# Low halves of weights and operand pairs made by an accumulating DMA in place of VectorE differences

## The chip, the cores and the metric

The kernel runs on one core of one Trainium2 chip. The metric is the time of one execution on the device in microseconds; the verdict compares medians of several runs. In the profile PE is TensorE (PEld its weight loads), DVE is VectorE, ACT is ScalarE, POOL is GpSimd, and SP is the engine whose queue issues most loads.

## The reference

A trunk of two layers over 512 tokens of 1024 channels in float32. Each layer has a mixing part (a combined projection, four branches, gates, an output projection, a residual add), and behind it a feed-forward part, in which the change lies:

```python
def _conv_ffn(h, w_up, conv_w, conv_b, w_down):
    u = _depthwise_conv(h @ w_up, conv_w, conv_b)      # width 3, along the tokens
    gate, up = jnp.split(u, 2, axis=-1)
    return (jax.nn.silu(gate) * up) @ w_down
...
x = x + _conv_ffn(_rmsnorm(x, g_ffn[l]), w_up[l], ffn_conv_w[l], ffn_conv_b[l], w_down[l])
```

`w_up` is 1024 x 5632 (22 blocks of 128 gate channels and 22 of up channels), `w_down` is 2816 x 1024.

## The kernel before

**Products in two halves.** TensorE works on the type fp32r, which keeps fewer bits than float32. Each operand x is therefore split: a high part hi = x rounded to fp32r, and a low part lo = x - hi. A product is three matmuls, hi*hi, hi*lo and lo*hi, summed in PSUM (`prod`, lines 291 to 296). ScalarE makes the high part by a copy, VectorE makes the low part by a subtraction.

**Weights.** `weights` (line 243) prepares the entries of `w_list` in their order, always two ahead of the one in use (`unit`, `LOOK = 2`). For a plain entry it loads 512 KB on SP's queue into `w_raw` (two buffers), makes `w_hi` on ScalarE (line 273) and `w_lo` on VectorE (line 275); `w_hi` and `w_lo` have three buffers each, so the tile of block k can be written when TensorE is done with block k-3. An entry is a pair (n, pieces); n is 1024 for plain blocks, 0 for entries of the down-projection, and 'seven' for the entries below, which `seven_unit` prepares (lines 1276 and 1277), where further operands are added to a raw tile in place by an accumulating DMA on GpSimd's queue (`grow`, line 1258).

**Up-projection.** `ffn` (line 1190) walks `UP_STEPS`. Blocks 2 to 15 are computed in pairs of blocks by a seven-product scheme (`seven`, line 1111); blocks 0, 1 and 16 to 21 are whole: `block` (line 312) makes 24 matmuls of 512 columns for the gate half (s = 0) and the same for the up half (s = 1). VectorE takes each result from its bank into `U` (line 1215); there are four banks named mm and four named aux. Then `conv_part` (line 1163) does the width-3 convolution: one ScalarE step (line 1171) and two VectorE steps (1172, 1173), for s = 0 a Silu on ScalarE (1177), for s = 1 the product with it (1185). The result for blocks 2j and 2j+1 lies side by side in one tile `f` with the tag `fp{j}`, 128 x 1024.

**Down-projection.** `down` (line 1369) also works by seven products, on pairs j = 0 to 10. Each needs operands made from f by `split_pair` (line 1329): four VectorE steps of 256 columns (sums and differences of the quarters of the two blocks), and splits into hi and lo of both blocks, of the sum tile `a` (512 columns) and of a quarter `b` (256 columns): ScalarE at line 1354, VectorE at line 1355. Pairs 0 to 5 are done early, still in the up-projection, behind blocks 15 to 20 (`EARLY`); pairs 6 to 10 at the start of the first steps of `down`. The low parts of pair j go into the buffer of the pair before, `fp{j-1}`; those of pair 0 into the tag `lo`.

**What sets the order.** Tile, the framework, fixes the order of instructions on each engine when the kernel is built, by priorities: work on weights comes with a high priority (`high_priority`), and engines run their list in that order and wait at semaphores. A buffer with a tag is written again only after its last reader is done.

Of the kernel before, what the change touches and what calls it, by code (L numbers as in the profile page):

```python
# [14 lines left out]
F32 = mybir.dt.float32  # L15
F32R = mybir.dt.float32r
I32 = mybir.dt.int32
AF = mybir.ActivationFunctionType
ALU = mybir.AluOpType
# [3 lines left out]
P = 128  # L23
L = 2
D = 1024
S = 512
KT = D // P
NB = S // P
DFF = 2816
# [31 lines left out]
              ('gb', 'A22'), ('ga', 'S2'), ('ga', 'S1'), ('gb', 'S2'), ('gb', 'S1'), ('ga', 'S4'), ('gb', 'S4')]  # L61
MIX = (0, 1, 4, 5, 2, 3, 6, 7)

EARLY = (15, 16, 17, 18, 19, 20)
EPS = 1e-6
BIG = 1e30
EB = 4
# [167 lines left out]
class Trunk:  # L235
# [7 lines left out]
    def weights(self, upto, ahead=3000, parts=1, queue=None):  # L243

        nc = self.nc
        while self.w_emitted < min(upto, len(self.w_list)):
            n, pieces = self.w_list[self.w_emitted]
            if n == 'seven':
                with self.tc.high_priority(offset=ahead):
                    self.w_ready.append(self.seven_unit(*pieces))  # L250
                self.w_emitted += 1
                continue
            with self.tc.high_priority(offset=ahead):

                self.w_fast = (self.w_fast + 1) % 4 if n == 0 else 0
                if n == 0 and self.w_fast in (3, 0):
                    raw = self.fp.tile([P, 1024], F32, name="w_raw", tag="w_more", bufs=2)
                else:
                    raw = self.wpool.tile([P, 1024], F32, name="w_raw", tag="w_raw", bufs=2)
                hi = self.wpool.tile([P, 1024], F32R, name="w_hi", tag="w_hi", bufs=3)  # L260
                lo = self.wpool.tile([P, 1024], F32R, name="w_lo", tag="w_lo", bufs=3)
                src = pieces()
                n = sum(p.shape[1] for p in src)
                if len(src) == 1:
                    cut = [slice(i * n // parts, (i + 1) * n // parts) for i in range(parts)]
                    src = [src[0][:, s] for s in cut]
                c = 0
                for p in src:
                    (queue or nc.sync).dma_start(raw[:, c:c + p.shape[1]], p)
                    c += p.shape[1]  # L270
                for i in range(parts):
                    s = slice(i * n // parts, (i + 1) * n // parts)
                    w = nc.scalar.activation(hi[:, s], raw[:, s], AF.Copy)  # L273
                    self.first_hi = self.first_hi or w
                    nc.vector.tensor_tensor(lo[:, s], raw[:, s], hi[:, s].bitcast(F32), ALU.subtract)  # L275
            self.w_ready.append((hi, lo))
            self.w_emitted += 1

# [884 lines left out]
    def conv_part(self, i, s):  # L1163

        nc = self.nc
        v = nc.vector
        c = i + s * NF
        u = self.U[s][:, i % 2]
        y = self.fp.tile([P, S], F32, name=f"cy{s}", tag=f"cy{s}", bufs=2)
        w = lambda t: self.par('ffn_conv_w', c * 3 + t)  # L1170
        nc.scalar.activation(y, u[:, 1:513], AF.Identity, scale=w(1), bias=self.par('ffn_conv_b', c))  # L1171
        v.scalar_tensor_tensor(y, u[:, 0:512], w(0), y, ALU.mult, ALU.add)
        v.scalar_tensor_tensor(y, u[:, 2:514], w(2), y, ALU.mult, ALU.add)

        if s == 0:
            si = self.fp.tile([P, S], F32, name="fth", tag="fth", bufs=2)
            nc.scalar.activation(si, y, AF.Silu)
            self.silus[i] = si
            return
        if self.last and i % 2 == 1 and i // 2 < KT:  # L1180
            self.turn_res(i // 2)
        if i % 2 == 0:
            self.fpair = self.fp.tile([P, 1024], F32, name="f", tag=f"fp{i // 2}", bufs=1)
        fl = self.fpair[:, i % 2 * S:(i % 2 + 1) * S]
        v.tensor_tensor(fl, y, self.silus.pop(i), ALU.mult)
        self.F.append(fl)
        if i in EARLY:
            self.split_pair(self.F, EARLY.index(i), self.got)

    def ffn(self, l, last):  # L1190
        nc = self.nc
        v = nc.vector
        self.U = []
        for i in range(2):
            u = self.conv_tile(f"U{i}")
            nc.gpsimd.memset(u[:, :, 0:1], 0.0)
            nc.gpsimd.memset(u[:, :, 513:514], 0.0)
            self.U.append(u)
        self.F, self.got, self.silus, self.sevens, self.last = [], {}, {}, {}, last
        held = {}  # L1200
        self.pace = 0.0
        for kind, a, b in UP_STEPS:
            if kind == 'seven':
                self.seven(a, b)
                continue
            if kind == 'free':
                ps = held.pop((a, b))
            else:
                ps = self.mm()
                self.block(ps)  # L1210
                self.tick()
            if kind == 'held':
                held[a, b] = ps
            else:
                v.tensor_tensor(self.U[b][:, a % 2, 1:513], ps, self.RB, ALU.mult)  # L1215
                self.conv_part(a, b)
        for g in self.slow:
            for _ in g:
                pass
        self.slow = []  # L1220
        return self.F
# [107 lines left out]
    def split_pair(self, F, j, got):  # L1329

        nc = self.nc
        v = nc.vector
        fi, fk = F[2 * j:2 * j + 2]

        def tile(t):
            if isinstance(t, tuple):
                t, n = t
                if n == 0:
                    pool = self.fp2 if t[:2] == "lt" else self.fp
                    self.halves[t] = pool.tile([P, 1024], F32R, name=f"p{t}", tag=t, bufs=1)  # L1340
                return self.halves[t][:, n * S:(n + 1) * S]
            pool = self.xpool if t[:2] in ("xh", "xl") else self.fp2 if t[:2] in ("fh", "t2", "t3") else self.fp
            return pool.tile([P, S], F32R, name=f"p{t}", tag=t, bufs=2 if t in ("lo", "xr", "xn", "cy0", "cy1") else 1)

        tags = self.pair_tags(j)
        ih, kh, il, kl, ah, al = (tile(t) for t in tags[:6])
        if j % 2 == 0:
            got['b'] = [tile(t) for t in tags[6:]]
        lo, hi = slice(0, 256), slice(256, 512)
        bh, bl = (t[:, (lo, hi)[j % 2]] for t in got['b'])  # L1350
        a = self.fp.tile([P, S], F32, name="sum", tag="xr" if j < len(EARLY) else "fth", bufs=2)

        def split(h, l, x):
            nc.scalar.activation(h, x, AF.Copy)
            v.tensor_tensor(l, x, h.bitcast(F32), ALU.subtract)

        v.tensor_tensor(a[:, lo], fi[:, hi], fk[:, hi], ALU.subtract)
        v.tensor_tensor(fi[:, hi], fi[:, lo], fi[:, hi], ALU.subtract)
        v.tensor_tensor(a[:, hi], a[:, lo], fi[:, lo], ALU.subtract)
        split(ih, il, fi)  # L1360
        split(ah, al, a)
        split(kh, kl, fk)
        v.tensor_tensor(fk[:, lo], fk[:, lo], a[:, hi], ALU.add)
        split(bh, bl, fk[:, lo])
        cut = lambda h, l, c: [(h[:, c + b * P:c + (b + 1) * P], l[:, c + b * P:c + (b + 1) * P]) for b in range(2)]
        got[j] = {'a11': cut(ih, il, 0), 's1': cut(ih, il, 256), 'a12': cut(kh, kl, 0), 's4': cut(kh, kl, 256),
                  's3': cut(ah, al, 0), 's2': cut(ah, al, 256), 'a22': cut(bh, bl, 0)}

    def down(self, F, last):
# [9 lines left out]

        got, todo = self.got, list(range(len(EARLY), NP2))  # L1380
        A, B = ([self.mm() for _ in range(2)] for _ in range(2))
# [94 lines left out]
    def run(self):  # L1476
        nc, tc = self.nc, self.tc
        with ExitStack() as st:
            pool = lambda name, **k: st.enter_context(tc.tile_pool(name=name, bufs=1, **k))
# [9 lines left out]
            for l in range(L):  # L1489
                off, quads, quarters, ups, mixing = 0, [], {}, {}, []  # L1490
                for kind, a, n in UNITS:
                    src = self.W[l, off:off + n * P].rearrange("(p c) -> p c", p=P)
# [16 lines left out]
                for kind, a, b in UP_STEPS:  # L1509
                    if kind == 'seven':  # L1510
                        self.w_list.append((kind, (l, a, b)))
                    elif kind != 'free':
                        self.w_list.append((1024, lambda src=ups[b * DFF + a * P]: [src]))
                self.quarters.append(quarters)
                self.quads.append(quads)
                self.sums.append([])
# [12 lines left out]
            with tc.tile_pool(name="first", bufs=1, reuse_waits="tile") as first:  # L1529
# [11 lines left out]
                for d in range(KT):  # L1541
                    if d == 0:
                        xn = x0[:, KT:]
                        for s in (slice(0, KT + 256), slice(KT + 256, KT + S)):
                            nc.sync.dma_start(x0[:, s], self.X0[:, s])
                    else:
                        xn = first.tile([P, S], F32, name="xn", tag="xn", bufs=7)
# [163 lines left out]
```

## Time and profile before

| | |
|---|---|
| median of 3 runs | 1548.46 us (1544.78 to 1549.47) |
| the profiled execution | 1549.1 us, span of its instructions 1547.3 us |
| granted TensorE clock | 1.000 |
| GpSimd issues of line 1258 | 72 (54 into chain, 18 into w_raw) |
| loads of 512 KB into w_raw on SP's queue | 187 of W, median 4.4 us to landing |
| HBM read / written | 258.20 MB / 58.72 MB |

Busy time is the time in which an engine has an instruction under way, so stages with different limits are averaged in the page's first line; the windows by stage tell them apart. A busy TensorE may still be held up between two matmuls by less than the view shows, as the ends of matmuls are modelled. The time to landing runs from the start of the issuing instruction to the transfer's last semaphore event.

### The profile page before, as it was taken

The page shows a single profiled execution, that of the slowest core. Times are in us where ns is not written, and L with a number is a line of the kernel's source. Part 1 is how long each engine was busy: PE and PEld are TensorE (multiplying, and loading weights), DVE is VectorE, ACT ScalarE, POOL GpSimd, SP SyncE. Part 2 cuts the span into 40 slices and gives each one's busy share as a digit, 9 for nine tenths or more (in the row PEclk, how much of TensorE's full clock was granted, in tenths as well). Part 3 has the DMA queues.
Part 4 walks back from the last instruction along what each step waited for, and adds up shares of the span by engine and source line. Part 5 has one row for each costly group of instructions (what it writes and reads, how often), then busy time and mean ns, then how long its engine had stood idle before and what let it go on. Part 6 is the DMA issues. An engine that isn't in the chain of part 4 may idle for free.

```text
span 1547.3 us, 23306 instructions
## 1 busy us (share of the span) xinstructions
PE 1530.9 (99%) x8446; PEld 1325.7 (86%) x8446; DVE 1308.3 (85%) x2220; ACT 953.0 (62%) x1600; POOL 185.9 (12%) x280
## 2 busy tenths in 40 slices
PE   9999999999999999999999999999999999999998
PEld 8888888889889998878888888888898899998787
DVE  6689988797879989996576899887988789999974
ACT  6677777356655666564548687673566565665643
POOL 0123002220001110000002130023200011100000
PEclk9999999999999999999999999999999999999999
DMA  7789586756558886366558796866665699863664
GB/s 233 235 224 200 164 177 157 177 153 152 177 142 179 190 169 159 95 209 198 180 184 254 206 197 175 170 160 182 147 152 177 171 216 213 173 164 95 188 223 157
DMA packets 116739, 277.57 MB, mean 179 GB/s; under 512 B 27280, under 2 KB 29200, under 8 KB 116624
## 3 DMA queue, kind: packets, MB, share of 16 engines
q1 hardware_dynamic: 86800, 186.93, 37.7%
q0 software_dynamic: 29536, 88.62, 31.1%
q8 instruction: 67, 1.10, 0.3%
q10 hardware_dynamic: 288, 0.52, 0.1%
q14 instruction: 48, 0.39, 0.1%
HBM read 258.20 MB, written 58.72 MB: 205 GB/s over the span
## 4 chain that ended last, share of the span: by engine, by line
PE 69%; DVE 16%; DMA 6%; ACT 5%; issue 4%; SPq 0%; POOL 0%; ACTq 0%; DVEq 0%; POOLq 0%
PE mm L294 11%; PE mm L295 11%; PE mm L296 11%; PE aux L1128 5%; DVE w_lo L1277 4%; DMA chain<-W 4%; PE aux L948 3%; PE aux L1378 3%; PE aux L1377 3%; PE aux L1376 3%; DVE w_lo L275 2%; PE mm L1376 2%; PE mm L1378 2%; PE mm L1377 2%; DMA w_raw<-W 2%
## 5 line engine op out<-in xcount | busy, mean ns | idle before, releaser
L273 ACT ACTIVATE w_hi<-w_raw 128x1024 fp32r<-128x1024 f32 (+1 forms) x233 | 241.9, 1041 | 198.1 <-PE aux L1378 51.0
L275 DVE TENSOR_TENSOR w_lo<-w_raw,w_hi 128x1024 fp32r<-128x1024 f32 (+1 forms) x233 | 280.5, 1206 | 72.5 <-ACT w_hi L273 71.3
L294 PE MATMUL mm<-xh,w_hi 128*128 128x512 f32 x704 | 275.6, 391 | 0.0
L295 PE MATMUL mm<-xl,w_hi 128*128 128x512 f32 x704 | 274.6, 390 | 0.0
L296 PE MATMUL mm<-xh,w_lo 128*128 128x512 f32 x704 | 274.5, 390 | 0.0
L1128 PE MATMUL aux<-form,w_hi 128*128 128x256 f32 x896 | 160.8, 280 | 0.7 <-ACT sv L1140 0.7
L296 PEld LDWEIGHTS mm<-xh,w_lo 128*128 128x128 f32 x704 | 132.2, 188 | 28.3
L294 PEld LDWEIGHTS mm<-xh,w_hi 128*128 128x128 f32 x704 | 132.2, 188 | 26.3
L295 PEld LDWEIGHTS mm<-xl,w_hi 128*128 128x128 f32 x704 | 132.3, 188 | 25.9
L1128 PEld LDWEIGHTS aux<-form,w_hi 128*128 128x128 f32 x896 | 137.5, 188 | 1.7 <-ACT sv L1140 1.1
L1128 PE MATMUL aux<-form,w_lo 128*128 128x256 f32 x448 | 125.9, 281 | 0.0
L1277 DVE TENSOR_TENSOR w_lo<-chain,w_hi 128x1024 fp32r<-128x1024 f32 x72 | 87.9, 1220 | 32.2 <-ACT w_hi L1276 28.6
L1276 ACT ACTIVATE w_hi<-chain 128x1024 fp32r<-128x1024 f32 x72 | 76.0, 1056 | 61.4 <-DMA chain<-W 27.8
L469 DVE SCALAR_TENSOR_TENSOR cv<-cv,prm 128x512 f32<-128x512 f32 x120 | 94.7, 789 | 0.7
L1171 ACT ACTIVATE cy<-U,prm 128x512 f32<-128x512 f32 x88 | 67.9, 808 | 40.6 <-DVE U L1215 30.3
L1258 POOL DMA_DIRECT2D chain<-W x54 | 47.3, 876 | 328.9 <-DVE w_lo L1277 296.8
L1128 PEld LDWEIGHTS aux<-form,w_lo 128*128 128x128 f32 x448 | 84.1, 188 | 0.4 <-DVE w_lo L1277 0.4
L1276 ACT ACTIVATE w_hi<-w_raw 128x1024 fp32r<-128x1024 f32 x54 | 56.7, 1054 | 43.8 <-PE aux L1128 18.2
L532 PE MATMUL mm<-w_hi,xh 128*128 128x512 f32 x192 | 76.4, 398 | 0.3 <-DVE V L660 0.3
L533 PE MATMUL mm<-w_lo,xh 128*128 128x512 f32 x192 | 74.9, 390 | 0.0
L534 PE MATMUL mm<-w_hi,xl 128*128 128x512 f32 x192 | 74.9, 391 | 0.0
L1277 DVE TENSOR_TENSOR w_lo<-w_raw,w_hi 128x1024 fp32r<-128x1024 f32 x54 | 65.8, 1219 | 6.0 <-ACT w_hi L1276 4.6
(372 smaller groups left out, 3900.2 us busy)
## 6 DMA issues: line engine op xcount, KB each, us to landing
w_raw<-W SPq DMA_DIRECT2D x187, 512.0 KB, 4.4
chain<-W POOLq DMA_DIRECT2D x54, 512.0 KB, 5.7
sums<-W POOLq DMA_DIRECT2D x24, 1024.0 KB, 12.0
w_raw<-W SPq DMA_DIRECT2D x66, 256.0 KB, 3.8
w_raw<-sums SPq DMA_DIRECT2D x44, 256.0 KB, 3.8
w_raw<-sums SPq DMA_DIRECT2D x22, 512.0 KB, 4.3
sums<-W POOLq DMA_DIRECT2D x12, 768.0 KB, 10.3
chain<-W SPq DMA_DIRECT2D x18, 512.0 KB, 5.0
```

Source lines behind the costliest of these rows:

```text
L273: w = nc.scalar.activation(hi[:, s], raw[:, s], AF.Copy)
L275: nc.vector.tensor_tensor(lo[:, s], raw[:, s], hi[:, s].bitcast(F32), ALU.subtract)
L294: mm(ps, lhsT=wh, rhs=xh, start=start, stop=False)
L295: mm(ps, lhsT=wh, rhs=xl, start=False, stop=False)
L296: self.last_mm = mm(ps, lhsT=wl, rhs=xh, start=False, stop=stop)
L469: self.after_mm(v.scalar_tensor_tensor(acc, u[:, t:t + S], w(t), acc, ALU.mult, ALU.add))
L1128: self.last_mm = nc.tensor.matmul(o, lhsT=w[:, s], rhs=x, start=start and not (e or j or i), stop=j == 3 and i == 2, skip_group_check=True)
L1276: nc.scalar.activation(hi, raw, AF.Copy)
L1277: nc.vector.tensor_tensor(lo, raw, hi.bitcast(F32), ALU.subtract)
L1376: mm(ps, lhsT=x[0], rhs=w[0][:, cols], start=start, stop=False, skip_group_check=again)
L1377: mm(ps, lhsT=x[0], rhs=w[1][:, cols], start=False, stop=False, skip_group_check=again)
L1378: self.last_mm = mm(ps, lhsT=x[1], rhs=w[0][:, cols], start=False, stop=stop, skip_group_check=again)
```

## The change

Two groups of low parts are no longer VectorE differences. ScalarE writes minus the high part into the low tile, and an accumulating DMA on GpSimd's queue adds the original values to it, from HBM for weights and from the tile f in SBUF for pairs: lo = -hi + x.

The weights are those of the whole blocks 18 to 21, both halves, in each layer: their entry carries n = 2 in place of 1024, and `weights` reads it as a flag.

The pairs are the six early ones. `early_pair` replaces `split_pair` for them: one high part of 128 x 1024 in place of two of 128 x 512, one negation, one DMA. The quarter b is written to a further tile of the tag `xr` and no longer into f, which the DMA reads. `EARLY` now names the block and the half behind which a pair is made: pair 1 moves from behind block 16 to behind the first half of block 17.

```diff
-EARLY = (15, 16, 17, 18, 19, 20)
+EARLY = ((15, 1), (17, 0), (17, 1), (18, 1), (19, 1), (20, 1))
...
-                src = pieces()
+                src, summed = pieces(), n == 2
...
                     w = nc.scalar.activation(hi[:, s], raw[:, s], AF.Copy)
                     self.first_hi = self.first_hi or w
-                    nc.vector.tensor_tensor(lo[:, s], raw[:, s], hi[:, s].bitcast(F32), ALU.subtract)
+                    if summed:
+                        nc.scalar.activation(lo[:, s], hi[:, s].bitcast(F32), AF.Copy, scale=-1.0)
+                        nc.gpsimd.dma_start(lo[:, s], src[i], accum_op=ALU.add)
+                    else:
+                        nc.vector.tensor_tensor(lo[:, s], raw[:, s], hi[:, s].bitcast(F32), ALU.subtract)
...
             self.silus[i] = si
+            if (i, 0) in EARLY:
+                self.early_pair(EARLY.index((i, 0)))
...
-        if i in EARLY:
-            self.split_pair(self.F, EARLY.index(i), self.got)
+        if (i, 1) in EARLY:
+            self.early_pair(EARLY.index((i, 1)))
+
+    def early_pair(self, j):
+
+        nc = self.nc
+        v = nc.vector
+        f = self.fpairs[j]
+        tags = self.pair_tags(j)
+        hi = self.fp2.tile([P, 1024], F32R, name="pfh", tag=f"fh{j}", bufs=1)
+        low = self.fp.tile([P, 1024], F32R, name="plo", tag=f"fp{j - 1}" if j else "lo", bufs=1)
+        ah, al = (self.pair_tile(t) for t in tags[4:6])
+        if j % 2 == 0:
+            self.got['b'] = [self.pair_tile(t) for t in tags[6:]]
+        bh, bl = (t[:, j % 2 * 256:j % 2 * 256 + 256] for t in self.got['b'])
+        a = self.fp.tile([P, S], F32, name="sum", tag="xr", bufs=2)
+        q = lambda n: f[:, n * 256:(n + 1) * 256]
+        v.tensor_tensor(a[:, :256], q(1), q(3), ALU.subtract)
+        v.tensor_tensor(q(1), q(0), q(1), ALU.subtract)
+        nc.scalar.activation(hi, f, AF.Copy)
+        nc.scalar.activation(low, hi.bitcast(F32), AF.Copy, scale=-1.0)
+        nc.gpsimd.dma_start(low, f, accum_op=ALU.add)
+        v.tensor_tensor(a[:, 256:], a[:, :256], q(0), ALU.subtract)
+        b = self.fp.tile([P, S], F32, name="sum", tag="xr", bufs=2)[:, :256]
+        v.tensor_tensor(b, q(2), a[:, 256:], ALU.add)
+        nc.scalar.activation(ah, a, AF.Copy)
+        v.tensor_tensor(al, a, ah.bitcast(F32), ALU.subtract)
+        nc.scalar.activation(bh, b, AF.Copy)
+        v.tensor_tensor(bl, b, bh.bitcast(F32), ALU.subtract)
...
-                        self.w_list.append((1024, lambda src=ups[b * DFF + a * P]: [src]))
+                        self.w_list.append((2 if a >= 18 else 1024, lambda src=ups[b * DFF + a * P]: [src]))
```

`pair_tile` is the function `tile` that stood inside `split_pair`, moved out so that both can use it; `split_pair` still serves pairs 6 to 10. `fpairs` is a list of the tiles f. `pair_tags`, which names the buffers, is unchanged.

More of the change, by code (lines that the diff above doesn't have):

```diff
@@ L1183, in conv_part @@
             self.fpair = self.fp.tile([P, 1024], F32, name="f", tag=f"fp{i // 2}", bufs=1)
+            self.fpairs.append(self.fpair)
         fl = self.fpair[:, i % 2 * S:(i % 2 + 1) * S]
@@ L1186, in conv_part @@
         self.F.append(fl)
-        if i in EARLY:
-            self.split_pair(self.F, EARLY.index(i), self.got)
+        if (i, 1) in EARLY:
[25 more added lines that the diff above has]
+        v.tensor_tensor(bl, b, bh.bitcast(F32), ALU.subtract)
+        cut = lambda h, l, c: [(h[:, c + b * P:c + (b + 1) * P], l[:, c + b * P:c + (b + 1) * P]) for b in range(2)]
+        self.got[j] = {'a11': cut(hi, low, 0), 's1': cut(hi, low, 256), 'a12': cut(hi, low, 512),
+                       's4': cut(hi, low, 768), 's3': cut(ah, al, 0), 's2': cut(ah, al, 256), 'a22': cut(bh, bl, 0)}
@@ new lines, in pair_tile @@
+    def pair_tile(self, t):
+        if isinstance(t, tuple):
+            t, n = t
+            if n == 0:
+                pool = self.fp2 if t[:2] == "lt" else self.fp
+                self.halves[t] = pool.tile([P, 1024], F32R, name=f"p{t}", tag=t, bufs=1)
+            return self.halves[t][:, n * S:(n + 1) * S]
+        pool = self.xpool if t[:2] in ("xh", "xl") else self.fp2 if t[:2] in ("t2", "t3") else self.fp
+        return pool.tile([P, S], F32R, name=f"p{t}", tag=t, bufs=2 if t in ("xr", "xn", "cy0", "cy1") else 1)
@@ L1199, in ffn @@
         self.F, self.got, self.silus, self.sevens, self.last = [], {}, {}, {}, last
+        self.fpairs = []
         held = {}
@@ L1333, in split_pair @@
         fi, fk = F[2 * j:2 * j + 2]
[L1335 to L1343, printed above, removed]
+        tile = self.pair_tile
         tags = self.pair_tags(j)
```

## The prediction

> **What bounds the kernel now.** I read the page's busy line first, then busy time by stage, then the end of the up-projection instruction by instruction.
>
> ```profile
> span 1547.3 us, 23306 instructions
> PE 1530.9 (99%) x8446; PEld 1325.7 (86%) x8446; DVE 1308.3 (85%) x2220; ACT 953.0 (62%) x1600; POOL 185.9 (12%) x280
> q0 software_dynamic: 29536, 88.62, 31.1%
> ```
>
> TensorE is busy for all but 1547.3 - 1530.9 = 16.4 us, so nothing that relieves another engine can return more than that, and only where the wait ends there. The stages that the edit touches are the end of the up-projection (606 to 664 us in layer 0, 1374 to 1437 in layer 1) and the down-projection behind each. The next rows give, after each window, its length, the busy time of PE, PEld, DVE, ACT and POOL, the granted clock, the share of the 16 DMA engines, and GB/s.
>
> ```profile
> 450.00:600.00 150.00, 148.96 (x1187) 145.58 (x1186) 133.31 (x171) 92.83 (x116) 23.61 (x27) 1.00 0.81 178
> 606.00:664.00 58.00, 58.00 (x269) 48.51 (x268) 57.94 (x94) 34.62 (x51) 0.00 (x0) 1.00 0.34 101
> 612.00:658.00 46.00, 46.00 (x205) 38.10 (x204) 45.96 (x76) 23.26 (x35) 0.00 (x0) 1.00 0.34 102
> 664.00:724.00 60.00, 59.19 (x258) 48.11 (x257) 51.90 (x91) 34.74 (x46) 0.00 (x0) 1.00 0.68 222
> 1374.00:1437.00 63.00, 63.00 (x291) 52.62 (x290) 62.94 (x102) 39.65 (x59) 0.00 (x0) 1.00 0.35 109
> 1437.00:1497.00 60.00, 59.74 (x260) 48.48 (x259) 50.06 (x75) 33.92 (x44) 0.00 (x0) 1.00 0.68 212
> ```
>
> VectorE is full there (57.94 of 58, 62.94 of 63), but TensorE never waits: 58.00 of 58, 63.00 of 63. VectorE keeps up exactly. The list of TensorE's waits shows where its backlog surfaces, and what else TensorE waits for on VectorE:
>
> ```profile
> PE aux L948 <- DVE w_lo L1277: 3.1, 4, 0.8
> ...
> PE aux L1128 <- DVE w_lo L1277: 1.3, 3, 0.6
> ...
> PE mm L1376 <- DVE U L1215: 1.1, 2, 0.8
> ```
>
> The third row is the one: at the start of each down-projection a product needs a bank that VectorE empties late, two waits, 1.1 us in all. The other two lie in stages that the edit leaves alone.
>
> **VectorE, what goes.** The groups of 606 to 664 us, one row for each kind of work:
>
> ```profile
> L275 DVE TENSOR_TENSOR w_lo<-w_raw,w_hi 128x1024 fp32r<-128x1024 f32 x11 | 13.4, 1218 | 0.0
> L1355 DVE TENSOR_TENSOR pfp<-f,pfh 128x512 fp32r<-128x512 f32 x9 | 6.0, 683 | 0.0
> L273 ACT ACTIVATE w_hi<-w_raw 128x1024 fp32r<-128x1024 f32 x11 | 11.5, 1047 | 1.3 <-PE mm L295 1.3
> L1354 ACT ACTIVATE pfh<-f 128x512 fp32r<-128x512 f32 x7 | 4.3, 627 | 5.5 <-DVE f L1358 5.5
> ```
>
> Eight blocks (18 to 21, both halves) a layer lose 1.218 us each: 9.7. Six pairs lose two differences of 0.683 each: 8.2. The other VectorE steps of a pair keep their count and size. So 17.9 us a layer leave an engine that has none to spare, and the backlog at the down-projection goes: I credit both of its waits, -1.1 us. Next behind it is the product's own rate; nothing more comes back here, because TensorE waits for nothing else.
>
> **ScalarE, what is added.** Eight negations of 1.047 us (8.4), and for each pair two instructions of 1.047 in place of two of 0.627 (6 x 0.84 = 5.0): 13.4 us, so 48.0 of 58. It fits; 13.4 us of ScalarE's idle time there was waiting for VectorE, by the same list:
>
> ```profile
> L1171 ACT ACTIVATE cy<-U,prm 128x512 f32<-128x512 f32 x14 | 10.9, 810 | 13.4 <-DVE U L1215 12.8 <-DVE U L1153 0.7
> ```
>
> **GpSimd's queue and the latency of a weight.** GpSimd is idle in the stage (0.00) and gets 14 issues a layer. The nearest rows are the growing operand sums of line 1258, also accumulating DMAs of 512 KB into SBUF:
>
> ```profile
> L1258 POOL DMA_DIRECT2D chain<-W x54: 863/872/909, 328.8 to 1361.4; - x54
> ...
> DMA to landing us min/median/max: 5.1/5.7/9.8
> ```
>
> 14 x 0.872 = 12.2 us of issuing, hidden. The landing isn't free: the low part now comes 1.047 + 5.7 us after the high part, where it was 1.218. Low-part tiles rotate over three buffers, so block k's is free when block k-3 is done, and its first use is the third product of block k:
>
> ```profile
> 615.28 1.06 ACT L273 ACTIVATE w_hi<-w_raw 128x1024 fp32r<-128x1024 f32 x1 [1.31 <-PE mm L295]
> 626.59 0.39 PE L296 MATMUL mm<-xh,w_lo 128*128 128x512 f32 x1
> 632.96 1.05 ACT L273 ACTIVATE w_hi<-w_raw 128x1024 fp32r<-128x1024 f32 x1
> 642.91 0.39 PE L296 MATMUL mm<-xh,w_lo 128*128 128x512 f32 x1
> ```
>
> First pair of rows: 615.28 + 1.06 + 1.05 + 5.7 = 623.1, needed at 626.59, 3.5 us to spare. Second, where ScalarE comes late: 640.8 against 642.91, 2.1 to spare. So a median landing hides; the longest seen (9.8) would stop TensorE by 0.6 to 2.0 us. I use 2.8 us as the mean slack.
>
> The Trainium skill would put this landing lower: "DMA: Bandwidth & Descriptors", section "Anatomy of one DMA — SWDGE (gpsimd) path", fits 2.0 us plus bytes / 436 GB/s, 3.2 us for 512 KB. By that the slack is 5.3 us and the sum is -1.1 us. The 5.1 to 9.8 us above speak against it for accumulating transfers.
>
> **The DMA engines.** This decides the sign. A window with one accumulate and nothing else large, one with a plain load of the same 512 KB, and a crowded one:
>
> ```profile
> 330.40:334.20 3.80, 3.80 (x19) 3.18 (x19) 3.23 (x5) 3.00 (x4) 0.00 (x0) 1.00 0.88 141
> 618.50:621.70 3.20, 3.20 (x16) 2.65 (x15) 3.20 (x6) 2.17 (x3) 0.00 (x0) 1.00 0.56 164
> 1251.00:1260.00 9.00, 9.00 (x78) 9.00 (x78) 8.53 (x12) 6.61 (x10) 2.62 (x3) 1.00 1.04 214
> ```
>
> The accumulate holds all 16 engines for 0.88 x 3.80 = 3.34 us, a plain load for 0.56 x 3.20 = 1.79. Three values for an accumulate: 3.34 alone; 2.85 from the software queue's line (88.62 MB in 31.1% of 1547.3 us is 184 GB/s, but plain copies are among them); and from 450 to 600 us, where 27 of them share the engines with loads: 178 GB/s x 150 us = 26.7 MB, less 14.2 MB of accumulates leaves 12.5 MB of loads, at 164/0.56 = 293 GB/s 42.8 us; (0.81 x 150 - 42.8) / 27 = 2.91 us. I take 2.91, since that stage is the most alike. A pair's accumulate reads SBUF where these read HBM; no row shows one. Bounds: 1.79, the plain load, and 3.34.
>
> The accumulates that the products wait for, or that lie ahead of those in the queue, are the eight weights and the pairs between the first and the last (four of six; the first can go before, the sixth is wanted in the down-projection). They fall into 612 to 658 us: 12 x 2.91 = 34.9 us, and 0.34 x 46 = 15.6 us are there already: 50.5 us of work in 46. Short by 4.5, of which 2.8 is slack: 1.7 us of stall a layer, 3.4 in both. With 2.85: 49.8, 1.0 a layer. With 3.34: 55.7, 6.9 a layer. With pairs at 1.79: 8 x 2.91 + 4 x 1.79 + 15.6 = 46.0, none. The crowded window, at a share of 1.04, kept PE at 9.00 of 9, so a short overload is carried.
>
> Of waits that the edit adds: a pair's negation writes the buffer of the pair before, so it waits until that pair's DMA has landed, and ScalarE's next high part is queued behind it. Blocks are (642.91 - 626.59) / 3 = 5.44 us apart, negation and landing take 1.05 + 5.7 = 6.7, and only pairs 1 and 2 are one block apart: 1.3 us, inside the 2.1, nothing. GpSimd's queue has nothing else that waits. In the down-projection the share is 0.68, with room for the last pair. Pair 1 moves from block 16 to the first half of block 17, one product later, and its first use is two weight tiles into the down-projection: nothing. On SP's queue the next raw load can start earlier, since ScalarE's high part is now the raw tile's last reader: nothing, loads land before they are wanted (ScalarE waits for PE in the row at 615.28, not for a load).
>
> **Sum.** -1.1 + 3.4 = +2.3 us: 1549.1 for the profiled execution (span 1547.3 and 1.8 around it) becomes 1551.4; the median of the runs shown, 1548.46, is 0.6 lower, so 1550.8. A measurement here tells about 0.3% from no change, 4.6 us: my forecast is "within", at +0.15%.
>
> **Rivals**, each from the median 1548.46.
> Slower, the DMA engines fill. Same place, 612 to 658 us and its twin in layer 1, with 3.34 us for each accumulate: 2 x 6.9 - 1.1 = +12.7 us, 1561.2. It leaves the 0.3% when an accumulate costs more than (46 + 2.8 + 2.85 - 15.6) / 12 = 3.0 us, close to my 2.91. For it: 3.34 was measured alone, and pairs queue ahead of weights in one queue. Against: 2.91 was measured in company, and 1.04 did no harm. The Trainium skill's rule behind it, "DMA: Bandwidth & Descriptors", section "Issuing engines are not separate DMA queues", is that all issuers' transfers run interleaved on the same 16 engines; the crowded window's share agrees. Chance 0.34.
>
> Slower, ScalarE blocked. With a landing of 9.8 us between pairs 1 and 2 it stands 1.05 + 9.8 - 5.44 = 5.4 us, 3.3 over the slack, a layer: +6.6 - 1.1 = +5.5, 1554.0. For it: the order on ScalarE is fixed ahead of the run. Against: one place a layer. Chance 0.05.
>
> Slower, GpSimd held off. If each issue had to wait out one VectorE instruction of 1.218 us, the slack would be 1.6 and the stall 2 x (4.5 - 1.6): 5.8 - 1.1 = +4.7, 1553.2. Against: 863 to 909 ns for each of 54 issues, in stages where VectorE is busy for 133.31 of 150 us. The Trainium skill has the rule that speaks for it, in "SBUF — State Buffer", section "Who interferes with whom": a VectorE instruction with two inputs in SBUF contends with GpSimd's reads there. These issues show none of it. Chance 0.02.
>
> No stall at all: pairs near a plain load's price, -1.1 us, 1547.4. It is within 0.3% as well. Of the chance 0.52 for "within", I give 0.2 to this and 0.32 to the forecast.
>
> Faster: no stall, and the freed VectorE brings a new order of the instructions behind, which also removes both w_lo rows above: -1.1 - 3.1 - 1.3 = -5.5, 1543.0. For it: layer 1 follows the edit. Against: those waits lie 400 us and more behind layer 0's, or ahead of it. Chance 0.07. That the edit does not act is not likely: the flag is read only where those blocks are loaded, and both names of the pairs are rewired; it would give 1549.
>
> **Numbers.** Likeliest 1550.8. "Within" holds 0.52, from 1543.8 to 1553.1; its own range is 1546 to 1553. The slower cases hold 0.41, from 1553 to beyond 1561, the faster 0.07. For 8 in 10 I reach from 1545 to 1561.5.
>
> **What would show it.** In 606 to 664 us: VectorE near 40 us in place of 57.94, ScalarE near 48, 14 GpSimd issues, a DMA share of 0.9 and more. The wait at L1376 gone. If I am right on the stalls, TensorE waits on landing low parts a few times a layer, each under 2 us. I am wrong if those waits add up to over 6 us, with landings of 8 us and more (engines full); if ScalarE stands still at a pair's negation with weights queued behind; or if TensorE shows no new wait and the time falls by more than 2 us, which would mean gain from a stage that I call untouched.

## The result

The changed kernel takes 1561.41 us, median of 4 runs (1560.22 to 1563.33), beside 1548.97 us for the kernel before in the same session (1544.78 to 1550.23, 4 runs). The ratio is 1.0086, interval 1.0063 to 1.0109: slower by 0.9%, some 13 us, more than the 0.3% that a measurement tells. The forecast was "within 0.3%", 1550.8. The time is that of the first rival (engines full, 1561.2); whether its cause is, too, the runs had to show.

The profiled execution of the changed kernel, its busy line and the software queue:

```profile
span 1558.5 us, 23328 instructions
PE 1533.1 (98%) x8446; PEld 1325.9 (85%) x8446; DVE 1279.8 (82%) x2180; ACT 977.8 (63%) x1616; POOL 210.8 (14%) x308
q0 software_dynamic: 33568, 103.30, 35.6%
```

VectorE gave up 1308.3 - 1279.8 = 28.5 us and the span grew by 1558.5 - 1547.3 = 11.2 us. The same stages as before, in the same columns (length, busy time of PE, PEld, DVE, ACT and POOL, granted clock, DMA share, GB/s):

```profile
450.00:600.00 150.00, 149.36 (x1190) 146.03 (x1189) 133.08 (x170) 92.89 (x115) 23.62 (x27) 1.00 0.81 178
606.00:664.00 58.00, 53.55 (x244) 43.51 (x243) 44.96 (x79) 45.46 (x59) 11.41 (x13) 1.00 0.96 217
612.00:658.00 46.00, 41.55 (x180) 33.09 (x179) 34.97 (x64) 39.30 (x51) 11.41 (x13) 1.00 0.96 217
664.00:724.00 60.00, 59.93 (x262) 48.69 (x261) 47.68 (x83) 34.24 (x44) 0.00 (x0) 1.00 0.66 217
1374.00:1437.00 63.00, 56.82 (x278) 47.30 (x277) 50.07 (x85) 49.87 (x64) 12.31 (x14) 1.00 0.89 210
```

450 to 600 us is untouched. In the two edited stages TensorE, which was busy throughout, now stands 58.00 - 53.55 = 4.5 us and 63.00 - 56.82 = 6.2 us. The down-projection behind is a little fuller than before (59.93 for 59.19). TensorE's longest waits say for what (us in total, times, longest):

```profile
PE mm L300 <- DMA w_lo<-W: 10.6, 7, 3.6
PE aux L952 <- DVE w_lo L1325: 3.0, 4, 0.8
```

Line 300 is the third product, the first to use a weight's low part, and the wait is for the accumulating DMA that fills it. The forecast's third row, the bank that VectorE emptied late, is gone from the list. So 10.6 - 1.1 = 9.5 of the 11.2 us is in these waits; I did not trace the rest. Of the 10.6 us, 4.4 are in layer 0 and 6.2 in layer 1.

Two more views show what lies ahead of those products. The first is the weights' accumulate by source line (when the first and the last were issued, who waited for them, and their landing), the second ScalarE's idle time at a pair's negation:

```profile
L277 POOL DMA_DIRECT2D w_lo<-W x16: 872/875/975, 615.8 to 1434.5; - x16
...
  PEld mm L300: 14.1, 8
  PE mm L300: 10.6, 7
...
DMA to landing us min/median/max: 6.0/7.4/9.2
```

```profile
its engine sat idle before it (us, times) until:
  DMA plo<-f: 10.1, 7
```

A weight lands 7.4 us after its issue, not 5.7; and ScalarE stood 10.1 us in front of negations, each until the DMA of the pair before had read the buffer that the negation overwrites. Two explanations offered themselves. **Engines full:** 28 accumulates more make every landing late. **ScalarE stands:** the hold at a pair's negation delays the weights' own negations, queued behind it. A third was that the longer chain (negation, issue, landing) is too long by itself.

### The profile page after: what moved, and what is told of

Read it like the earlier page. It is cut to its first block, busy times and chain, and to the rows that moved or that the text cites. A ratio compares the mean times of both kernels' runs of the same rounds, so it can differ in the third digit from the quotient of the medians.

```text
span 1558.5 us, 23328 instructions
## 1 busy us (share of the span) xinstructions
PE 1533.1 (98%) x8446; PEld 1325.9 (85%) x8446; DVE 1279.8 (82%) x2180; ACT 977.8 (63%) x1616; POOL 210.8 (14%) x308
## 4 chain that ended last, share of the span: by engine, by line
PE 68%; DVE 15%; DMA 8%; ACT 4%; issue 4%; POOL 0%; ACTq 0%; DVEq 0%; POOLq 0%
PE mm L300 10%; PE mm L298 10%; PE mm L299 10%; PE aux L1132 5%; DVE w_lo L1325 4%; PE aux L952 3%; DMA chain<-W 3%; PE aux L1417 3%; PE aux L1415 3%; PE aux L1416 3%; PE mm L536 2%; PE mm L537 2%; PE mm L538 2%; DMA plo<-f 2%; PE mm L1417 2%
## 5 line engine op out<-in xcount | busy, mean ns | idle before, releaser
L279 DVE TENSOR_TENSOR w_lo<-w_raw,w_hi 128x1024 fp32r<-128x1024 f32 (+1 forms) x217 | 261.1, 1205 | 80.5 <-ACT w_hi L273 79.4
L300 PE MATMUL mm<-xh,w_lo 128*128 128x512 f32 x704 | 275.5, 391 | 10.7 <-DMA w_lo<-W 10.6
L1176 DVE SCALAR_TENSOR_TENSOR cy<-U,prm,cy 128x512 f32<-128x512 f32 x88 | 63.2, 746 | 21.0 <-ACT cy L1175 21.0
```

What stands on the lines that cost most here:

```text
L300: self.last_mm = mm(ps, lhsT=wl, rhs=xh, start=False, stop=stop)
```

## The experiments

Each kernel starts from the changed one, and the diff shows what differs from it. Ratios are to the kernel before on the same chip.

### One half at a time

`w_only` keeps the DMAs for the weights and gives the pairs one VectorE difference of 1024 columns each:

```diff
-        nc.scalar.activation(low, hi.bitcast(F32), AF.Copy, scale=-1.0)
-        nc.gpsimd.dma_start(low, f, accum_op=ALU.add)
+        v.tensor_tensor(low, f, hi.bitcast(F32), ALU.subtract)
```

> Only the eight weight blocks a layer use the accumulating DMA; the pairs' low part is a VectorE difference of 1024 columns again. Theory engines full: 8 x 3.1 us of accumulates and 15.6 us of loads are 40 us in the 46 us window, so no stall: time of before within 2 us, landing of the weights near 5.7 to 6.2 us, share of the DMA engines near 0.85. Theory ScalarE held at the pairs' negations: no such negations, so also before within 2 us. Third theory, the chain high part, negation, DMA is too long for three buffers by itself: TensorE still waits at the low part, 4 to 6 us of the 10.6 remain, before + 4 to 6.

1546.71 us, ratio 0.9989 [0.9979, 1.0000]. TensorE waits for no low part that a DMA makes. The window of layer 0, with all eight transfers, and the landings of both layers:

```profile
612.00:658.00 46.00, 46.00 (x204) 38.10 (x203) 43.90 (x75) 36.32 (x48) 7.01 (x8) 1.00 0.85 192
```

```profile
DMA to landing us min/median/max: 5.4/6.0/7.6
```

The third explanation falls for these blocks: the same chain, alone, hides. The pairs, or the company of both, cost the time.

`p_only` is the other half: the weights are VectorE differences again, the pairs use their DMAs:

```diff
-                        self.w_list.append((2 if a >= 18 else 1024, lambda src=ups[b * DFF + a * P]: [src]))
+                        self.w_list.append((1024, lambda src=ups[b * DFF + a * P]: [src]))
```

> Only the six pairs a layer use the accumulating DMA; the weights are VectorE differences again and have some 7 us to spare. Engines full: 4 x 3.1 + 15.6 = 28 us in 46, no stall, before - 1 us. ScalarE held: it still stands at the pairs' negations (some 10 us in all), but the weights' slack hides it: before within 1.5 us. Chain too long: nothing, before - 1.

1560.04 us, ratio 1.0067 [1.0045, 1.0088]: as slow as the whole, but by another wait, which no theory had. TensorE's wait first; then, in order of time, GpSimd's issue for the last early pair, VectorE's first split of the next pair, and the product that waited:

```profile
PE mm L1415 <- DVE U L1263: 7.7, 2, 4.8
```

```profile
662.13 0.87 POOL L1215 DMA_DIRECT2D plo<-f  x1 [8.93 <-DVE cy L1176]
```

```profile
668.46 0.69 DVE L1394 TENSOR_TENSOR pfp<-f,pxl 128x512 fp32r<-128x512 f32 x1 [2.29 <-DMA plo<-f]
...
672.11 0.68 DVE L1263 TENSOR_TENSOR U<-mm,RB 128x512 f32<-128x512 f32 x1
```

```profile
672.85 0.79 PE L1415 MATMUL mm<-w_hi,pe 128*128 128x512 f32 x1 [4.76 <-DVE U L1263]
```

With the weights on VectorE again, pair 5's steps come late. Its DMA goes out at 662.13 (652.55 in the changed kernel) and still reads f when VectorE wants to write the next pair's low part there. VectorE stands 2.29 us, the evacuation of the bank is queued behind, and TensorE stands 4.76. It is the old wait at the entry of the down-projection, made worse. `p_five` tests that by giving pair 5 alone a VectorE difference:

```diff
-        nc.scalar.activation(low, hi.bitcast(F32), AF.Copy, scale=-1.0)
-        nc.gpsimd.dma_start(low, f, accum_op=ALU.add)
+        if j == 5:
+            v.tensor_tensor(low, f, hi.bitcast(F32), ALU.subtract)
+        else:
+            nc.scalar.activation(low, hi.bitcast(F32), AF.Copy, scale=-1.0)
+            nc.gpsimd.dma_start(low, f, accum_op=ALU.add)
```

> The pairs' half alone (weights by VectorE differences), with pair 5's low part by a VectorE difference too and pairs 0 to 4 by DMA. If VectorE held up behind pair 5's late DMA at the entry of the down-projection is what cost the pairs' half 11 us: that wait for the bank (7.7 us) and the slow-clock stretches behind it go, time 1546 to 1549. If it is the pairs' transfers as such: still over 1555.

1550.56 us, ratio 1.0019 [1.0006, 1.0031]. Most of the loss goes with that one transfer, but not all: 3.9 us of the same wait are left, so the time is between the two expectations. VectorE no longer waits for a DMA there, but it runs without a gap from 657.42 to the evacuation at 667.81: it is behind. It lost time some 50 us earlier. ScalarE stands at pair 1's negation, a weight's high part is queued behind that, and VectorE waits for it (ScalarE's row, then VectorE's):

```profile
612.70 1.06 ACT L1217 ACTIVATE plo<-pfh 128x1024 fp32r<-128x1024 f32 x1 [2.63 <-DMA plo<-f]
```

```profile
614.74 1.23 DVE L279 TENSOR_TENSOR w_lo<-w_raw,w_hi 128x1024 fp32r<-128x1024 f32 x1 [2.72 <-ACT w_hi L273]
```

In `neither`, which has no such hold, VectorE waits for nothing from 606 to 668 us and TensorE's wait is absent. The 2.7 us are close to the 2.4 that TensorE waits in this layer; no run takes this hold alone away. Pairs beside a full VectorE are no gain. This kernel also prices a pair, four of whose transfers lie whole in the window, and `neither` (below) has none:

```profile
612.00:658.00 46.00, 46.00 (x204) 38.09 (x204) 43.08 (x72) 31.12 (x41) 3.50 (x4) 1.00 0.56 147
```

(0.56 - 0.32) x 46 / 4 = 2.76 us of all 16 engines.

### The order alone, and the relief alone

`neither` has the new order of a pair's steps but VectorE differences everywhere (both diffs above):

> The new order of a pair's steps (pair 1 half a block later, differences of 1024 columns in place of two of 512), with no DMA for any low part. If the order itself costs or gains something, it shows here: I expect none, 1547 to 1549, with TensorE's wait for the bank that VectorE empties at the entry of the down-projection still there.

1547.46 us, ratio 0.9995 [0.9986, 1.0005]. I expected the wait at the entry of the down-projection to stay, and it is no longer in the list of TensorE's waits. The order is worth nothing that can be measured in time, but that wait goes with it, without any relief of VectorE.

```profile
612.00:658.00 46.00, 46.00 (x204) 38.10 (x203) 45.98 (x74) 25.51 (x34) 0.00 (x0) 1.00 0.32 105
```

`no_add` is the whole change with the two `dma_start(..., accum_op=ALU.add)` lines taken out:

> All of the change without the 28 accumulating DMAs: every low part stays minus the high part, so the addition is left out. It gives the value of VectorE's relief alone, with ScalarE's added work in place. As predicted for that term: about 1.1 us below the kernel before, 1547; if freed VectorE is worth more in stages that I called untouched: under 1545; if ScalarE's 13.4 us more a layer cost something: 1549 or more.

1544.52 us, ratio 0.9980 [0.9969, 0.9991]: 1.4 to 4.8 us for VectorE's relief, where 1.1 was forecast. ScalarE's added steps cost nothing that shows in the time. This is about what the change could have brought with its transfers free. Its window gives the loads without accumulates:

```profile
612.00:658.00 46.00, 46.00 (x205) 38.09 (x204) 38.34 (x67) 38.72 (x52) 0.00 (x0) 1.00 0.34 110
```

With w_only's 0.85, eight weights cost (0.85 - 0.34) x 46 / 8 = 2.93 us each; with the 0.32 of `neither` for the loads it would be 3.05. The forecast's 2.91 was close, and pairs cost nearly the same.

### Load against standing

`p_short` is the whole change with a sixteenth of the pairs' bytes:

```diff
-        nc.gpsimd.dma_start(low, f, accum_op=ALU.add)
+        nc.gpsimd.dma_start(low[:, :64], f[:, :64], accum_op=ALU.add)
```

> All of the change, but each pair's DMA adds only 64 of its 1024 columns (the rest of the low part is left as minus the high part, so that work is left out). Same instructions on ScalarE, same count of DMAs, a sixteenth of the pairs' bytes. Engines full or ScalarE standing on a long pair's transfer: no wait on the weights' low parts, time as with the weights' half alone or a little below, about 1546. If the count of GpSimd's DMAs or the two extra ScalarE steps were the cause: waits stay, over 1555.

1545.80 us, ratio 0.9993 [0.9980, 1.0005], and 0.6 us of waits on low parts. The count of DMAs and of ScalarE's steps is innocent: it is the length of the pairs' transfers. Both theories say so, and the next kernels were to part them.

`w_pads` is `w_only` with a copy of 1 MB from HBM to HBM on GpSimd's queue for each pair, which nobody waits for:

```diff
+        pad = self.dram.tile([P, 2048], F32, name="pad", tag=f"pad{j}", bufs=2)
+        self.paced(nc.gpsimd.dma_start(pad, self.all_quads[0][:P]))
```

> The weights use the accumulating DMA, the pairs a VectorE difference, and in place of each pair's accumulate GpSimd issues a copy of 1 MB from HBM to an unused place in HBM, at the same point and for nobody: work for the DMA engines (about 2 x 1.79 us each) without any wait on ScalarE. Engines full: landing of the weights 7 us and more, stalls at the low part of 6 to 14 us, before + 6 to + 14. ScalarE held: before within 2 us. Chain too long: as with the weights alone.

1554.31 us, ratio 1.0044 [1.0030, 1.0057]. Load alone makes stalls:

```profile
PE mm L300 <- DMA w_lo<-W: 5.1, 5, 1.9
```

```profile
612.00:658.00 46.00, 44.21 (x192) 35.51 (x191) 42.55 (x72) 35.31 (x46) 9.73 (x13) 1.00 1.01 292
```

The copies are the heavier load (a share of 1.01, where the changed kernel has 0.96) and bring half of its waits. `paced` makes each copy wait for a product, which does not hold the weights: behind each copy of layer 0 that a weight follows, GpSimd waited for ScalarE's negation.

`p_even` lets only pairs 0, 2 and 4 use DMAs, so that no negation waits for a transfer:

```diff
-        nc.scalar.activation(low, hi.bitcast(F32), AF.Copy, scale=-1.0)
-        nc.gpsimd.dma_start(low, f, accum_op=ALU.add)
+        if j % 2:
+            v.tensor_tensor(low, f, hi.bitcast(F32), ALU.subtract)
+        else:
+            nc.scalar.activation(low, hi.bitcast(F32), AF.Copy, scale=-1.0)
+            nc.gpsimd.dma_start(low, f, accum_op=ALU.add)
```

> All of the change, but pairs 1, 3 and 5 take a VectorE difference, so half of the pairs' DMAs are gone and no negation waits for the DMA of the pair before it, since that buffer's last reader is VectorE. Engines' load: 9 or 10 accumulates in the 46 us in place of 12, 43 us of work with the loads, below the limit: no stall, about 1547. If three pair transfers among the weights' are still too many: waits of 2 to 4 us, 1549 to 1552.

1555.36 us, ratio 1.0047 [1.0030, 1.0064]; the first expectation, which added up the engines' work as the forecast had, fell, and the second was too low. The waits, then the windows: layer 0, layer 1, and the longest late landing of layer 1.

```profile
PE mm L300 <- DMA w_lo<-W: 5.5, 6, 2.7
```

```profile
612.00:658.00 46.00, 45.02 (x196) 36.27 (x195) 40.06 (x70) 36.06 (x47) 8.74 (x10) 1.00 0.94 202
1386.00:1440.00 54.00, 49.92 (x219) 40.50 (x218) 45.24 (x76) 39.67 (x53) 8.76 (x10) 1.00 0.84 193
1417.00:1426.00 9.00, 6.62 (x30) 5.14 (x28) 7.38 (x14) 7.54 (x11) 1.74 (x2) 1.00 1.04 235
```

No negation waits for a DMA, and there are 5.5 us of stall: 1.4 in layer 0, at a share of 0.94, and 4.1 in layer 1, at a share of only 0.84. So the engines need not be over-full in the window as a whole. They are full while the late weights are under way: 1.04 in the last row, 0.99 from 1404 to 1412 us for the other. Three transfers among the weights' suffice to make a weight late by more than its slack. The longest wait is not load alone, though: ScalarE had stood 2.5 us for VectorE ahead of that weight, at pair 4's high part, and its DMA went out 6.0 us before the use and took 8.7.

`p_more` keeps all DMAs and takes ScalarE's wait away by other buffers:

```diff
-        low = self.fp.tile([P, 1024], F32R, name="plo", tag=f"fp{j - 1}" if j else "lo", bufs=1)
+        low = self.fp.tile([P, 1024], F32R, name="plo", tag=f"fp{j - 2}" if j > 1 else ("lo", "w_more")[j], bufs=1 + (j == 1))
```

> All of the change, with the same DMAs, but a pair's low part is written into the buffer of the pair two back (pair 1's into a tile that holds raw weights in other stages), so that ScalarE's negation no longer waits for the DMA of the pair just before. Engines full alone: TensorE's waits on the weights' low parts stay near 10.6 us, time about 1561. ScalarE's standing alone: no such wait, about 1547. Both, as the run with copies for nobody suggests (its waits were 5.1 us): ScalarE's wait on a pair's DMA falls below 2 us, TensorE's waits to about 5 us, time about 1554.

```profile
PE aux L1415 <- ACT w_hi L273: 20.4, 12, 2.5
PE mm L300 <- DMA w_lo<-W: 6.2, 7, 1.7
PE mm L1415 <- ACT w_hi L273: 3.8, 2, 2.2
```

ScalarE's wait at a negation is gone from the list, and TensorE's waits on low parts fall from 10.6 to 6.2 us, as expected of "both". In layer 0, which lies ahead of the disturbance named next, they fall from 4.4 to 2.2. The time, 1601.46 us (ratio 1.0342 [1.0303, 1.0380]), says nothing on that: the tile borrowed for pair 1 was wanted for raw weights, and TensorE waits 24.2 us for high parts in the down-projection.

`defer` gave pairs 1 to 5 their negation and DMA half a block to a block later, by a closure called from the block behind:

```diff
+        if (i, s) in ((17, 1), (18, 0), (19, 0), (20, 0), (21, 0)):
+            self.owed.pop(0)()
```

> All of the change, but the negation and the DMA of pairs 1 to 5 are given out half a block to a block later, behind the next block's last matmul, so that the DMA of the pair before has landed: the same work for the DMA engines, hardly any wait on ScalarE at the negation. Engines full: the stalls stay, 8 to 12 us at the low part, after within 3 us. ScalarE held: most of the stalls go, before + 1 to + 4. Chain too long: as after.

1569.58 us, ratio 1.0133 [1.0116, 1.0149]. The edit failed to do what it was for: negations still met transfers under way, and ScalarE stood longer.

```profile
ACT plo L1226 <- DMA plo<-f: 18.5, 6, 6.2
```

```profile
PE mm L300 <- DMA w_lo<-W: 16.4, 5, 4.7
```

It counts as a run with more standing: against the changed kernel 8.4 us more of it, and 5.8 us more stall at the same count of transfers. `p_short_pad` was to put the full load beside a ScalarE that doesn't wait: `p_short`, and behind each pair's DMA an accumulate of 512 KB into scratch:

```diff
+        self.paced(nc.gpsimd.dma_start(self.pads[j], self.all_quads[0][:P, :1024], accum_op=ALU.add))
```

> All of the change, with the pairs' DMAs of 64 columns as before (the rest of the add is left out), and behind each an accumulating DMA of 512 KB from HBM to a scratch tensor in HBM that nobody waits for. The engines' load of the whole change, with ScalarE's wait for a pair's transfer nearly gone. Engines' load alone explains the stalls: TensorE's waits on the weights' low parts 10 us or more, time about 1560. Load and ScalarE's standing each have their part, as the split of 6.2 and 4.4 us says: waits of 5 to 7 us, time about 1552 to 1555. ScalarE's standing alone: no waits, about 1546.

1577.83 us, ratio 1.0189 [1.0167, 1.0211], with 15.0 us of waits on low parts. It is inconclusive. `paced` makes the pad wait for a product, and GpSimd's queue with it; ScalarE still stood 6.9 us at negations, so the hold that the kernel was to remove was there.

```profile
POOL pad L1220 <- PE mm L300: 16.3, 7, 3.3
```

### Is there a faster version?

`w_again` is `w_only` once more with five rounds; `w_wide` is `w_only` with `a >= 16` for `a >= 18`.

> The weights' half alone once more, with more rounds, as the version that may beat both kernels: 1.5 to 2.5 us below the kernel before, about 1546; no wait of TensorE on a weight's low part.

1545.99 us, ratio 0.9988 [0.9976, 1.0000]. Twice the interval has just touched 1: perhaps 0.1% faster than before, at the edge of what can be told.

> The weights' half widened to blocks 16 to 21 (twelve weights a layer in place of eight), pairs by VectorE differences. By the engines' load (0.85 of them busy from 612 to 658 us with eight, the four more fall before 612, where the share is lower): no stall, 1545 to 1546, at most 1 us below the narrower one. If the stretch before 612 us is fuller than that: waits on low parts there, 1549 or more.

1571.14 us, ratio 1.0149 [1.0128, 1.0169]: the expectation was wrong by 25 us. Block 16 is mixed with the grown sums of the steps before, and its weight's high part is made only some 4 us ahead of use:

```profile
582.30 1.05 ACT L273 ACTIVATE w_hi<-w_raw 128x1024 fp32r<-128x1024 f32 x1
```

```profile
584.73 0.88 POOL L277 DMA_DIRECT2D w_lo<-W  x1 [2.07 <-ACT w_lo L276]
```

```profile
593.32 0.79 PE L300 MATMUL mm<-xh,w_lo 128*128 128x512 f32 x1 [6.51 <-DMA w_lo<-W]
```

```profile
586.00:593.00 7.00, 0.81 (x5) 0.45 (x4) 4.30 (x5) 2.89 (x4) 0.90 (x1) 0.92 1.03 224
```

TensorE wanted the low part at 593.32 - 6.51 = 586.81, 2.1 us after its DMA was issued, and the shortest landing in this kernel is 5.2 us: here the chain is too long by itself. The landing took 8.5 us, as the engines were full while it was under way (the last row), though their share from 580 to 606 us is 0.62.

## Why the prediction was wrong

**The failed step is the stall term, 3.4 us for 10.6.** It fell as a method more than by its price. The cost of an accumulate (2.91) is near what the runs give: 2.93 to 3.05 for a weight, 2.76 for a pair. The sum of work (50.5 us in 46, less slack) treats the window as one bucket, in which a transfer is late only when the engines overflow over its whole length. The runs show lateness without that: layer 1 of `p_even` stalls 4.1 us at a share of 0.84. What counts is each weight's own path in the seven to nine us from its issue to its landing, and the company that it meets there. The first stall of the changed kernel shows it on ScalarE, GpSimd and TensorE:

```profile
611.81 1.06 ACT L1214 ACTIVATE plo<-pfh 128x1024 fp32r<-128x1024 f32 x1 [1.61 <-DMA plo<-f]
612.78 1.04 ACT L273 ACTIVATE w_hi<-w_raw 128x1024 fp32r<-128x1024 f32 x1
...
614.43 1.05 ACT L276 ACTIVATE w_lo<-w_hi 128x1024 fp32r<-128x1024 f32 x1
```

```profile
615.77 0.88 POOL L277 DMA_DIRECT2D w_lo<-W  x1 [1.57 <-ACT w_lo L276]
```

```profile
622.94 0.50 PE L300 MATMUL mm<-xh,w_lo 128*128 128x512 f32 x1 [1.75 <-DMA w_lo<-W]
```

TensorE wanted the low part at 622.94 - 1.75 = 621.19, 5.4 us after the issue, and the landing took 7.1: 1.7 late. The same issue and the same product in `w_only`:

```profile
611.98 0.90 POOL L277 DMA_DIRECT2D w_lo<-W  x1 [25.09 <-DVE f L1212]
```

```profile
619.25 0.39 PE L300 MATMUL mm<-xh,w_lo 128*128 128x512 f32 x1
```

TensorE runs 1.8 us earlier there, so times of the two runs can't be compared as they stand, only the distance from issue to use. TensorE is free for the product at 619.41 (the end of the one before it), 7.4 us after the issue; the landing takes 5.5, so the part is 1.9 early. In the changed kernel the issue comes 7.4 - 5.4 = 2.0 us nearer to the use, and the landing takes 1.6 longer: 3.6 us in all, which eats the 1.9 and leaves the 1.7 of the stall. On ScalarE, 1.61 us of standing and the 1.06 of the pair's negation lie ahead of this weight. `p_more`, without the standing, has this issue 8.2 us ahead of the use, but the landing takes 8.6, and TensorE stands 0.4. So both theories hold for this stall: issue made late by ScalarE's order, and landing made late by company. While this transfer is under way the engines' share is 1.02, in `w_only` 0.88.

**Split of the 10.6 us.** `p_more` leaves 6.2 with all transfers and no standing, so 4.4 went with the standing. This is a split of waits in one trace for each; no run shows it in the total time, so how much of the 13 us each cause is worth stays open.

**The pair's negation ("inside the 2.1, nothing")** failed: 10.1 us of standing, at pairs 1, 3 and 4 of both layers and at pair 5 of layer 1, and none at pair 2, the one place that the forecast looked at. It lies in the same slack that the late landings were to be paid from. I had spent that slack twice. The second rival had the mechanism, but priced that one place.

**The landing ("a median landing hides")** was taken from a stage with other company. 7.4 us is this stage's median, and 1.7 more is most of the mean slack of 2.8.

**"A short overload is carried"** came from a window in which no product reads what an accumulate has just written: ScalarE and VectorE split it first (lines 1276 and 1277), and ScalarE there waits 1.0 us for a landing. It says nothing of transfers that a product waits for.

**First rival.** Its number, 1561.2, came from 3.34 us an accumulate, and by the runs' prices the mean of the twelve is 2.87 to 2.95, just under its condition (over 3.0). It had the place right and full engines as part of the cause; that the time agrees to 0.2 us is luck, as the standing took the place of the dearer price. For the profiled execution the forecast's sum was 1551.4; 4.4 us for the standing and 6.2 - 3.4 = 2.8 for late landing bring it to 1558.6 of the 1560.2 measured, and the last 1.6 are not traced.

**VectorE's relief** was mis-sized and partly for the wrong reason. The wait at the entry went, but `neither` loses it without any relief. The relief is worth 1.4 to 4.8 us by `no_add`, of which I had 1.1; where the rest comes back I did not follow up. VectorE gave up 28.5 / 2 = 14.3 us a layer for 17.9 in the sum (in the window 44.96 for "near 40"); partly because instructions in a row overlap, which a sum of durations counts twice (before, a weight's difference starts at 609.55, lasts 1.22, and the next step starts at 610.68). None of that shows in the time behind 10.6 us of stalls.

**Right:** ScalarE's load (45.46 for "near 48", in a window in which it also stood), GpSimd's 14 issues a layer at 0.875 us, unhindered by VectorE, so that the third rival falls; the DMA share (0.96); the order of pair 1; and the last pair. The latter was right in the whole change only; in `p_only`, where its DMA goes out 9.6 us later, it costs most of the loss.

## What to carry to other kernels

Where a product waits for a transfer, follow one operand from its first step to its use, with what is queued ahead on every engine it passes, and compare that with the lead; a sum of transfer time against a window can fit and the operand still be late. The engines' share over a long window hides the few us in which they are full. Slack is one sum: late landing, late issue and a wait of an engine in order are paid from the same few microseconds. An in-place reuse that is free behind a compute engine is a hold of many microseconds behind a DMA, so look for who stands in line behind the instruction that must wait; and half of a change may be worth keeping (weights alone, perhaps -0.1%) where the whole loses.

## What was not expected of the hardware

After longer stalls TensorE's granted clock fell to about half for some 4 us. The length, busy times, granted clock, share and GB/s of a window behind the stall, for `w_wide` (behind 6.51 us), `defer` (4.32), `p_only` (4.76) and `p_five` (2.35):

```profile
594.00:599.00 5.00, 5.00 (x14) 3.89 (x13) 1.17 (x2) 0.00 (x0) 0.00 (x0) 0.53 0.34 114
```

```profile
625.00:629.00 4.00, 4.00 (x12) 3.15 (x11) 3.96 (x8) 2.37 (x4) 0.00 (x0) 0.58 1.06 278
```

```profile
672.00:676.00 4.00, 3.15 (x8) 2.48 (x8) 4.00 (x7) 3.59 (x6) 0.00 (x0) 0.59 0.07 23
```

```profile
669.00:673.00 4.00, 4.00 (x13) 3.12 (x12) 4.00 (x6) 2.19 (x4) 0.00 (x0) 0.58 0.36 109
```

An undisturbed stage has 204 matmuls in 46 us, 0.225 us each. So the 14, 12 and 8 matmuls of the first three windows would have taken 3.2, 2.7 and 1.8 us of TensorE's 5.00, 4.00 and 3.15: 1.3 to 1.8 us lost on top of the stall, which is one reason why `p_only`, with 7.7 us of listed wait, lost more than that. The Trainium skill, "TensorE: Matmul & The Clock Gate", Part 1, has the rule: about 3.4 us of idling returns the array to half rate, and about as much sustained work restores it. The first three windows agree. The bound does not hold here as it stands: in `p_five` a wait of 2.35 us was enough for 0.58, while the changed kernel's longest, 3.6 us, was followed by a clock of 1.00. Why stays open.

```profile
1425.00:1430.00 5.00, 4.33 (x19) 3.60 (x20) 3.23 (x6) 3.94 (x6) 0.88 (x1) 1.00 1.05 212
```
